# Query and key preparation of a grouped-query layer: a fixed order over three tiles, doubled key heads, and score steps between the last products

## The chip, the cores and the metric

One Trainium2 chip, one of its cores. The metric is the device time of one execution in microseconds (us), lower is better. Times of several runs are given as median, lowest and highest; one more execution is profiled, and all rows of the profile are from that one.

The five engines run in parallel, each through its own list of instructions, in order: TensorE (PE; its weight loads are shown as PEld), VectorE (DVE), ScalarE (ACT), GpSimd (POOL) and SyncE (SP), which issues most DMA transfers. ScalarE's list issues DMA transfers too (ACTq). Matmuls write to PSUM, which has eight banks; GpSimd works on SBUF alone here.

## What is computed

One step of a two-layer trunk: 512 latent tokens and 128 context tokens ("prompt"), 1,024 channels, 16 heads of 64. Layer 0 mixes by neighbourhood attention, layer 1 by grouped-query attention with 4 key and value heads, each layer followed by a gated convolutional feed-forward. All is float32. The change is in layer 1's mixer, cut to what matters:

```python
def gqa_qkv(h, w_qkv, q_norm, k_norm):
    q, k, v = jnp.split(h @ w_qkv, [1024, 1024 + 256], axis=-1)
    q = rmsnorm(q.reshape(b, t, 16, 64), q_norm)     # per head
    k = rmsnorm(k.reshape(b, t, 4, 64), k_norm)
    return q, k, v.reshape(b, t, 4, 64)

qp, kp, vp = gqa_qkv(hp, ...)                        # 128 context tokens
op = blocked_attention(qp, kp, vp)                   # context reads context
qs, ks_, vs = gqa_qkv(hs, ...)                       # 512 latent tokens
qs, ks_ = axial_rope(qs), axial_rope(ks_)            # latents carry a position
k_all = concat([ks_, cache_gqa_k], axis=1)           # 512 + 128 cached context keys
v_all = concat([vs, cache_gqa_v], axis=1)
os_ = blocked_attention(qs, k_all, v_all)
x = x + gate * rmsnorm(concat(op, os_) @ w_o, norm_mix_post)
```

The context's normed keys and its values are outputs too (new_gqa_k, new_gqa_v).

## The kernel before

**Precision.** A float32 product is made of three passes in a faster type: each operand is split into a high part (cast) and a low part (the rest), and high x high, high x low, low x high are summed in PSUM. `wsplit` loads a weight block (raw tile `wr`), casts it on ScalarE (`wh`) and subtracts on DVE or, where told so, on GpSimd (`wl`). Tag `wr`, `wh`, `wl` have four buffers each in the pool `wp`.

**Order.** The tile framework's scheduler orders the instructions of every engine and places the waits. Two things bind it. All matmuls and transposes go through `pe()`, which chains each behind the one before it: TensorE's order is the order of the program text. And `tc.keep_in_program_order(ins)` puts an instruction behind the one written last for the same engine. Before the change only the output projection's weight splits are pinned that way; the rest of DVE, ScalarE and GpSimd is ordered by the scheduler's estimate. A buffer that takes the place of an earlier one waits until that one is no longer read.

**Preparation of layer 1's heads.** There are 15 tiles of 128 tokens x 512 columns: five for keys and values (tile t = 0 to 3 latent, 4 context), five for the query heads 0 to 7 (`hq` 0; order 4, 0, 1, 2, 3) and five for heads 8 to 15 (`hq` 1; order 0 to 4). Each goes through these steps:

- products (`products`): 24 matmuls of 512 columns into one bank (`gp`), two weight blocks of 256 rows per six of them. `after(u)` is called behind each quarter, u = 0 to 3
- statistics (`head_rms`): ScalarE squares (`sq`), DVE sums per head (`ssh`), GpSimd makes variance and reciprocal root (`vh`, `rh`)
- norm (`head_norm`): DVE multiplies by the root (`y`) and by the rotary table (`tab`, into `kt` or `qt`), four small products give the rotated half (`sq` again), GpSimd adds the two. Context tiles (t = 4) need only two multiplies
- turn (`turn_k`, `turn_q`): transposes on TensorE into a bank (`tk`, `tq`), then casts on ScalarE to the high part and differences on DVE to the low part (`gkh`, `gkl`, `gq`). Two readers of one bank are kept apart by the framework: the second cast follows the first difference

Keys are needed twice in the partitions (once for each of the two heads that share a query block), so `turn_k` writes each half twice, in pieces of 64 partitions:

```python
        for j in range(2):
            turn(tp[:, j * P : j * P + P], src[:, j * P : j * P + P], ident)
        for b in range(2):
            for part in (own, oth):
                nc.scalar.copy(kh[part, b::2, cols], tv[own])
            for part in (own, oth):
                nc.vector.tensor_sub(kl[part, b::2, cols], tv[own], f32(kh[own, b::2, cols]))
```

The table `tab` is made by DVE from `rot` (the rotation) and `gn` (the two gains, each also with its quarters swapped), which ScalarE's list loads by seven transfers; two more load the cached keys and values (`ck`, `cv`). Their buffers lie where layer 0's closing norm had its own.

The driver `step` calls for each tile products and statistics, then the norm of the tile before, then turns that are older: with `keep` = 1 those of the tile two back, for key tiles (`KP` = 2, 2, 2, 2, 1) three back. All of it stands behind the whole tile's products. Query weights are split while the fifth tile of the group before is multiplied, one block behind each quarter. Between query tiles stand steps of the context's own attention (`gqa_prompt`: scores, turn, values), at the tiles listed in `PSTEP`, counted from the first query tile.

**The units.** Then come 32 units (`Unit`): one head and 256 latent queries each. `scores(i)`: four matmuls of 320 keys into two banks (`s`), minimum on DVE (`nmg`), exponential on ScalarE (into `gp`, the sums read out behind it), reciprocal on DVE (`rcg`), scaling on GpSimd. `turns(j)` transposes (`tp`) and evicts (`pk`), `values` multiplies with v (`po`). Scores run two units ahead; those of units 0 and 1 stand in front of the loop. The loop's steps are in `GORDER`; "p" takes a waiting prompt step. Units need the keys of all tiles, but query heads only as their number comes up.

Of the kernel before, what the change touches and what calls it, by code (L numbers as in the profile page):

```python
# [9 lines left out]
F32 = mybir.dt.float32  # L10
# [47 lines left out]
PSTEP = (3, 5, 6, 6, 8, 9)  # L58
WU = 29
TP = 1  # L60
PSN = 4
# [4 lines left out]
KP = (2, 2, 2, 2, 1)  # L66
# [35 lines left out]
def hybrid_step(ctx: ExitStack, tc: tile.TileContext, A, O):  # L102
# [1265 lines left out]
    def gqa_w(c0, u, low=None):  # L1368
        return wsplit(rows(wqkv, 2 * u, 2, c0, 512), 2, 512, low)
# [20 lines left out]
    rot = ap.tile([P, 2, 4, HD], F32, name="rot", bufs=1)  # L1390
    nc.scalar.dma_start(rot, A["k_rope"])
# [9 lines left out]
    tab = ap.tile([P, 2, 2, 4, HD], F32, name="tab", bufs=1)  # L1401
    for i in range(2):
        for j in range(2):
            nc.vector.tensor_mul(tab[:, i, j], rot[:, j], gn[:, i, j].unsqueeze(1).broadcast_to([P, 4, HD]))

    last_rms = [None]

    def head_rms(src, n):

        sq = ap.tile([P, 8, HD], F32, tag="sq", name="sq")[:, 0:n, :]  # L1410
        nc.scalar.activation(sq, src, AF.Square)
        ss = sm.tile([P, 8], F32, name="ssh")[:, 0:n]
        nc.vector.tensor_reduce(ss, sq, axis=AX.X, op=ALU.add)
        v = sm.tile([P, 8], F32, name="vh")[:, 0:n]
        nc.gpsimd.tensor_scalar(v, ss, 1.0 / HD, EPS, op0=ALU.mult, op1=ALU.add)
        r = sm.tile([P, 8], F32, name="rh")[:, 0:n]
        last_rms[0] = nc.gpsimd.tensor_tensor(r, v, mhalf.broadcast_to([P, n]), op=ALU.pow)
        return sq, r

    def head_norm(dst, src, sq, r, t, i, n):  # L1420

        y = ap.tile([P, 8, HD], F32, tag="y", name="y")[:, 0:n, :]
        nc.vector.tensor_mul(y, src, r.unsqueeze(2).broadcast_to([P, n, HD]))
        if t == 4:
            nc.vector.tensor_mul(dst, y, gn[:, i, 0].unsqueeze(1).broadcast_to([P, n, HD]))
            return
        nc.vector.tensor_mul(dst, y, tab[:, i, 0, t].unsqueeze(1).broadcast_to([P, n, HD]))
# [3 lines left out]
        for b in range(2):  # L1431
            for a in range(2):
                nc.vector.tensor_mul(
                    s5[:, :, a, b, :], y5[:, :, a, 1 - b, :],
                    b4[:, a, b, :].unsqueeze(1).broadcast_to([P, n, 16]),
                )
        nc.gpsimd.tensor_add(dst, dst, sq)

    def put_v(c, src):
        nc.scalar.copy(vt[:, c], src.rearrange("p (a d) -> p a d", a=4))  # L1440

    def turn_k(src, cols):

        tp = bk.get("tk")
        for j in range(2):
            turn(tp[:, j * P : j * P + P], src[:, j * P : j * P + P], ident)
        tv = tp[:, 0:256].rearrange("p (a b) -> p a b", a=2)
        for b in range(2):
            own, oth = own_oth(b)
            for part in (own, oth):  # L1450
                nc.scalar.copy(kh[part, b::2, cols], tv[own])
            for part in (own, oth):
                nc.vector.tensor_sub(kl[part, b::2, cols], tv[own], f32(kh[own, b::2, cols]))
# [354 lines left out]
```

## Time and profile before

| | |
|---|---|
| median of 3 runs | 1630.63 us (1628.24 to 1637.93) |
| profiled execution | 1631.72 us, span 1629.9 us |
| mean granted TensorE clock | 0.986 |
| busy over the span | PE 96%, DVE 62%, ACT 53%, POOL 44% |
| stage of preparation | 874.7 to about 984 us |
| units | about 984 to 1125 us |

How to read the rows. A timeline row is start, duration, engine, line, operation, output <- input, count, and in brackets how long the engine was idle before and who ended that. A group's row has busy time, mean duration in ns, idle time before its instructions and its releaser; a tile's row has minimum, median and maximum duration in ns, then first and last start. A waits row is who waited, on whom, us in total, times, longest. A windows row has for a stretch of time the busy us and instructions of each engine, the granted TensorE clock (1.00 is full), the DMA share and GB/s. Matmuls overlap: a duration of 0.39 us goes with a start every 0.23 us.

### The profile page before, as it was taken

To read this page: it belongs to the slowest core of one execution; us is meant where nothing else is said; L and a number is where in the kernel's file an instruction comes from. 1 tells how busy PE (TensorE), PEld (TensorE's weight loads), DVE (VectorE), ACT (ScalarE), POOL (GpSimd) and SP (SyncE) were. 2 spreads that over 40 slices of the span, in tenths; PEclk is the share of its full clock that TensorE was granted. 3 is DMA by queue.
4 is the path that set the end of the run, shared out by engine and by line. 5 is a ranking of instruction groups with operands and counts; after the bars stand their busy time and mean duration, and the time that the engine had idled before them with its cause. 6 is when DMAs were issued, how large, how long until landed. Compare 5 with 4: busy or idle time off the path is not lost.

```text
span 1629.9 us, 26039 instructions
## 1 busy us (share of the span) xinstructions
PE 1557.0 (96%) x9709; PEld 1350.8 (83%) x9709; DVE 1011.8 (62%) x1645; ACT 858.0 (53%) x1641; POOL 723.0 (44%) x614
## 2 busy tenths in 40 slices
PE   5999999899999999999999997999999999999998
PEld 3888889778888888998887776777898999998886
DVE  3453534549866565775465877773787888885454
ACT  3464646545545454554444445763565656565433
POOL 1554545423253544544343355441524556563333
PEclk8999999999999999999999999999999999999999
DMA  9745553245466666348575110002635333338664
GB/s 286 184 138 143 137 143 73 63 135 176 147 199 214 196 204 207 103 161 299 197 235 178 60 39 14 1 1 101 220 114 187 117 103 109 107 115 285 209 210 140
DMA packets 193211, 242.42 MB, mean 149 GB/s; under 512 B 11100, under 2 KB 149564, under 8 KB 193084
## 3 DMA queue, kind: packets, MB, share of 16 engines
q1 hardware_dynamic: 182224, 233.13, 45.2%
q10 hardware_dynamic: 10860, 7.62, 2.7%
q8 instruction: 76, 1.25, 0.3%
q14 instruction: 51, 0.42, 0.1%
HBM read 214.38 MB, written 26.34 MB: 148 GB/s over the span
## 4 chain that ended last, share of the span: by engine, by line
PE 65%; DVE 12%; POOL 6%; DMA 6%; issue 5%; ACT 4%; SPq 1%; ACTq 0%; POOLq 0%; DVEq 0%
PE acc L114 18%; PE ux L114 10%; PE y L114 7%; PE qk L114 5%; PE uz L114 5%; PE s L114 4%; PE po L114 4%; PE tp L117 3%; PE vp L114 3%; DMA wr<-in_ada_w 3%; PE uy L114 3%; POOL wl L1099 2%; PE ada L114 2%; DVE t L1175 2%; DVE al L1099 1%
## 5 line engine op out<-in xcount | busy, mean ns | idle before, releaser
L167 POOL TENSOR_TENSOR wl<-wr,wh 128x1024 fp32r<-128x1024 f32 x75 | 183.7, 2452 | 267.1 <-ACT wh L165 260.6
L1099 POOL TENSOR_TENSOR wl<-wr,wh 128x1024 fp32r<-128x1024 f32 x80 | 194.6, 2451 | 55.5 <-ACT wh L1098 46.2
L114 PE MATMUL ux<-B,wh 128*128 128x322 f32 x832 | 201.9, 313 | 1.7 <-DVE B L220 1.6
L1175 DVE SCALAR_TENSOR_TENSOR t<-C,cw,t 128x644 f32<-128x644 f32 x176 | 156.5, 889 | 57.4 <-ACT t L1173 56.6
L114 PE MATMUL acc<-wh,alo 128*128 128x512 f32 x440 | 172.0, 391 | 0.0
L114 PE MATMUL acc<-wh,ahi 128*128 128x512 f32 x440 | 171.9, 391 | 0.0
L114 PE MATMUL acc<-wl,ahi 128*128 128x512 f32 x440 | 171.8, 391 | 0.0
L165 ACT CAST wh<-wr 128x1024 fp32r<-128x1024 f32 x140 | 145.3, 1048 | 32.9 <-DMA wr<-in_ffn_w_down 23.9
L114 PE MATMUL uz<-B,wh 128*128 128x322 f32 x640 | 158.5, 316 | 0.0
L114 PEld LDWEIGHTS ux<-B,wh 128*128 128x128 f32 x832 | 143.7, 189 | 9.4 <-issue 2.9
L1068 DVE TENSOR_TENSOR alo<-ain,ahi 128x384 fp32r<-128x384 f32 (+1 forms) x88 | 70.9, 815 | 95.7 <-ACT ahi L1066 95.4
L114 PE MATMUL ux<-B,wl 128*128 128x322 f32 x416 | 129.1, 310 | 0.0
L114 PE MATMUL qk<-hT,wh 128*128 128x384 f32 (+1 forms) x512 | 126.0, 319 | 0.3 <-DVE qs L776 0.2
L114 PEld LDWEIGHTS uz<-B,wh 128*128 128x128 f32 x640 | 111.8, 190 | 6.6 <-issue 3.7
L1099 POOL TENSOR_TENSOR vl<-wr,vh 128x1024 fp32r<-128x1024 f32 x38 | 96.8, 2547 | 36.4 <-ACT vh L1098 36.4
L1098 ACT CAST wh<-wr 128x1024 fp32r<-128x1024 f32 x88 | 89.6, 1050 | 33.1 <-DVE wr L1122 31.8
L1066 ACT CAST ahi<-ain 128x384 fp32r<-128x384 f32 (+1 forms) x88 | 40.2, 461 | 124.8 <-PE acc L114 91.7
L1173 ACT ACTIVATE t<-C,cw 128x644 f32<-128x644 f32 x88 | 78.7, 895 | 48.5 <-DVE C L1203 44.3
L114 PE MATMUL uz<-B,wl 128*128 128x322 f32 x320 | 100.2, 313 | 0.5 <-POOL wl L1099 0.4
L167 DVE TENSOR_TENSOR wl<-wr,wh 128x1024 fp32r<-128x1024 f32 x65 | 83.5, 1299 | 25.0 <-ACT wh L165 24.5
L114 PEld LDWEIGHTS acc<-wl,ahi 128*128 128x128 f32 x440 | 82.6, 188 | 18.0
L114 PEld LDWEIGHTS acc<-wh,ahi 128*128 128x128 f32 x440 | 82.6, 188 | 17.7
(249 smaller groups left out, 4009.4 us busy)
## 6 DMA issues: line engine op xcount, KB each, us to landing
wr<-in_ffn_w_up SPq DMA_DIRECT2D x88, 512.0 KB
wr<-in_ffn_w_down SPq DMA_DIRECT2D x88, 512.0 KB
wr<-in_ada_w SPq DMA_DIRECT2D x80, 512.0 KB
act<-act SPq DMA_DIRECT2D x44, 321.0 KB
wr<-in_na_w_qkv SPq DMA_DIRECT2D x24, 512.0 KB
mod<-modrow SPq DMA_DIRECT2D x20, 512.0 KB
ain<-act SPq DMA_DIRECT2D x44, 192.0 KB
wf<-in_ada_w SPq DMA_DIRECT2D x16, 512.0 KB
```

Source lines behind the costliest of these rows:

```text
L114: pe(nc.tensor.matmul(*a, **k))
L117: pe(nc.tensor.transpose(*a, **k))
L165: i = nc.scalar.copy(hi, raw)
L167: j = (low or nc.vector).tensor_sub(lo, raw, f32(hi))
L1066: nc.scalar.copy(hi[:, 0 : c1 - c0], ain[:, 0 : c1 - c0])
L1068: nc.vector.tensor_sub(lo[:, 0 : c1 - c0], ain[:, 0 : c1 - c0], f32(hi[:, 0 : c1 - c0]))
L1098: nc.scalar.copy(hl[0], src)
L1099: low.tensor_sub(hl[1], src, f32(hl[0]))
L1173: nc.scalar.activation(t, taps(0), AF.Identity, bias=cw[:, 3, n : n + 1], scale=cw[:, 1, n : n + 1])
L1175: nc.vector.scalar_tensor_tensor(t, taps(d), cw[:, w, n : n + 1], t, op0=ALU.mult, op1=ALU.add)
```

## The change

- The tile's steps become a class `Prep` with `products`, `stat`, `norm`, `turns`, and one loop runs over the 15 tiles. While tile i is multiplied, behind its first quarter: `stat` of i-1, `turns` of i-2 (and behind tile 2's first quarter also the cached keys' turn). Behind its last: `norm` of i-1. Every instruction of these steps on DVE, ScalarE and GpSimd is pinned (`o` is `tc.keep_in_program_order`).
- Query weight blocks are split earlier and pinned: block 0 of heads 0 to 7 behind tile 1, on GpSimd and in a pool of its own (`wx`); block 0 of heads 8 to 15 behind tile 6 (block 1 of these then takes `wx`); the others behind the first two quarters and the end of tiles 4 and 9, one of them on GpSimd.
- Keys: the norm writes each head twice side by side (`twice`), the cached keys are loaded twice; four transposes give both halves, then one cast and one difference over 128 partitions.
- The four score steps of units 0 and 1 move between the products of tiles 12 to 14 (`ESC`: tile and quarter to unit and step). Their exponentials go to `wr` buffers. The score banks are opened at tile 12, and the last 4 of the other banks are dropped there.
- Prompt steps stand at other tiles (`PSTEP` now counts from the first key tile). The last tile's turn and the opening of the attention output's buffers move behind unit 1.
- `rot` is loaded into a part of `tab`; the cached values are loaded straight to `vt`, without a copy.

```diff
-PSTEP = (3, 5, 6, 6, 8, 9)
+PSTEP = (8, 9, 10, 10, 11, 12)
+ESC = {(12, 2): (0, 0), (13, 1): (0, 1), (13, 3): (1, 0), (14, 2): (1, 1)}
-PSN = 4
-KP = (2, 2, 2, 2, 1)
...
+    o = tc.keep_in_program_order
     def head_rms(src, n):
-        nc.scalar.activation(sq, src, AF.Square)
+        o(nc.scalar.activation(sq, src, AF.Square))
...
-    def head_norm(dst, src, sq, r, t, i, n):
+    def head_norm(dst, src, sq, r, t, i, n, twice=None):
-        nc.vector.tensor_mul(y, src, r.unsqueeze(2).broadcast_to([P, n, HD]))
+        o(nc.vector.tensor_mul(y, src, r.unsqueeze(2).broadcast_to([P, n, HD])))
...
-        nc.gpsimd.tensor_add(dst, dst, sq)
+        if twice is not None:
+            dst, sq = (x.unsqueeze(2).broadcast_to([P, n, 2, HD]) for x in (dst, sq))
+        o(nc.gpsimd.tensor_add(dst if twice is None else twice, dst, sq))
...
     def turn_k(src, cols):
         tp = bk.get("tk")
-        for j in range(2):
-            turn(tp[:, j * P : j * P + P], src[:, j * P : j * P + P], ident)
...
+        for g in range(4):
+            turn(tp[:, g * P : g * P + P], src[:, g].rearrange("p a b -> p (a b)"), ident)
+        tv = tp.rearrange("p (a b) -> p a b", a=4)
+        o(nc.scalar.copy(kh[:, :, cols], tv))
+        o(nc.vector.tensor_sub(kl[:, :, cols], tv, f32(kh[:, :, cols])))
         bk.put(tp)
...
-    ck = ap.tile([P, 256], F32, tag="ck", name="ck", bufs=1)
-    nc.scalar.dma_start(ck, A["cache_gqa_k"][0, 0].rearrange("t h d -> t (h d)"))
-    cv = ap.tile([P, 256], F32, tag="cv", name="cv", bufs=1)
-    nc.scalar.dma_start(cv, A["cache_gqa_v"][0, 0].rearrange("t h d -> t (h d)"))
+    ck = ap.tile([P, 4, 2, HD], F32, name="ck", bufs=1)
+    for b in range(2):
+        nc.scalar.dma_start(ck[:, :, b, :], A["cache_gqa_k"][0, 0])
+    nc.scalar.dma_start(vt[:, 5], A["cache_gqa_v"][0, 0])
...
+    tiles = [Prep(None, t) for t in range(NT)]
+    tiles += [Prep(hq, t) for hq in range(2) for t in ((4, 0, 1, 2, 3), (0, 1, 2, 3, 4))[hq]]
+    group = [wkv, [], []]
+    for i, x in enumerate(tiles):
+        g = i // NT
+        def after(u):
+            if u == 0:
+                if i:
+                    tiles[i - 1].stat()
+                if i > 1:
+                    tiles[i - 2].turns()
+                if i == 2:
+                    turn_k(ck, slice(NS, T))
+            if i % NT == 4 and g < 2:
+                if u < 2:
+                    group[g + 1].append(gqa_w(512 * g, u + 1, (None, nc.gpsimd)[u], wx if g and u == 0 else None, True))
+            if (i, u) in ESC:
+                v, j = ESC[i, u]
+                if v not in un:
+                    un[v] = Unit(v)
+                un[v].scores(j)
+        if i == 10:
+            bk.first = psx
+        if i == 12:
+            bk.drop(4)
+            psy.close()
+            sps_p.append(sps.enter_context(pool("pss", space=PSUM)))
+        x.products(group[g], i % NT == 0, after)
+        if i:
+            tiles[i - 1].norm()
+        if i % NT == 4 and g < 2:
+            group[g + 1].append(gqa_w(512 * g, 3, None, None, True))
+        if i == 0:
+            late[0]()
+        elif i == 1:
+            late[1]()
...
+            group[1].append(gqa_w(0, 0, nc.gpsimd, wx, True))
+        elif i == 6:
+            group[2].append(gqa_w(512, 0, nc.gpsimd, None, True))
+        elif i == 7:
+            extra.extend(gqa_prompt(0) + gqa_prompt(1))
+        for _ in range(PSTEP.count(i)):
+            extra.popleft()()
+    bk.first = None
+    extra.extend(gqa_prompt(2) + gqa_prompt(3))
+    tiles[-1].stat()
+    tiles[-2].turns()
+    tiles[-1].norm()
...
-        for u in range(2):
-            for i in range(2):
-                un[u].scores(i)
         for u in range(NU + 2):
+            if u == 2:
+                tiles[-1].turns()
...
-                    if extra and (u == 0 or u >= PU0):
+                    if extra and u >= PU0:
                         extra.popleft()()
```

More of the change, by code (lines that the diff above doesn't have):

```diff
@@ L1389, in hybrid_step @@
     ap = gqs.enter_context(pool("gp", 2, "right"))
-    rot = ap.tile([P, 2, 4, HD], F32, name="rot", bufs=1)
-    nc.scalar.dma_start(rot, A["k_rope"])
+    wx = gqs.enter_context(pool("wx", 1, "right"))
+    tab = ap.tile([P, 2, 2, 4, HD], F32, name="tab", bufs=1)
+    nc.scalar.dma_start(tab[:, 1], A["k_rope"])
     gn = ap.tile([P, 2, 2, HD], F32, name="gn", bufs=1)
@@ new lines, in values @@
+    def values(two, cs):
+        u = two[0]
+        if cs[0] == 0 and u.hf == 0:
+            ta["po"] = bk.get("po")
+        for c in cs:
+            for v in two:
+                mm(ta["po"][64 * v.b : 64 * v.b + 64, 256 * u.hf : 256 * u.hf + 256],
+                   vt[:, c if c < 4 else 5, u.g, :], v.t[c], start=c == 0, stop=c == 4)
+        if cs[-1] == 4 and u.hf == 1:
+            p = u.p
+            hi, lo = osp1[p]
+            nc.scalar.copy(hi[:, 0:NS], ta["po"])
+            nc.vector.tensor_sub(lo[:, 0:NS], ta["po"], f32(hi[:, 0:NS]))
+            bk.put(ta["po"])
+            c, src = slice(NS, T), opr[:, p, :]
+            if p == KC - 1:
+                nc.scalar.copy(hi[:, c], src)
+                nc.vector.tensor_sub(lo[:, c], src, f32(hi[:, c]))
+            else:
+                i = nc.gpsimd.tensor_scalar(hi[:, c], src, 1.0, None, op0=ALU.mult)
+                nc.gpsimd.tensor_sub(lo[:, c], src, f32(hi[:, c]))
+                tc.add_manual_dep(i.ins, last_rms[0].ins.name, no_sync, reason="order")
@@ L1572, in hybrid_step @@
             late[0]()
-        elif t == 1:
+        elif i == 1:
             late[1]()
             xmp.close()
+            l_q = ExitStack()
+            lastq = l_q.enter_context(pool("q14", 1))
             pp_s = ExitStack()
             cur = [pp_s.enter_context(pool("prp", 1))]
-    turns.append(lambda: turn_k(ck, slice(NS, T)))
-    put_v(5, cv)
-    extra = deque()
-    for hq in range(2):
-        for n, t in enumerate(((4, 0, 1, 2, 3), (0, 1, 2, 3, 4))[hq]):
-            if hq and n == PSN:
-                bk.first = psx
-            step(q_tile(t, hq, wqs[hq], n == 0, ahead_of(1) if 5 * hq + n == 4 else None))
-            i = 5 * hq + n
-            if n == 2:
-                extra.extend(gqa_prompt(2 * hq) + gqa_prompt(2 * hq + 1))
-            for _ in range(PSTEP.count(i)):
-                extra.popleft()()
@@ L1591, in hybrid_step @@
-    step()
-    extra.extendleft(turns)
+            group[1].append(gqa_w(0, 0, nc.gpsimd, wx, True))
[10 more added lines that the diff above has]
+    tiles[-1].norm()
     pp_s.close()
-    hp2.close()
@@ L1595, in hybrid_step @@
     gqs.close()
     l_o1 = ExitStack()
-    op1 = l_o1.enter_context(pool("o1"))
-    osp1 = [[op1.tile([P, T], F32R, name=f"p{i}{p}") for i in "hl"] for p in range(KC)]
-    bk.first = None
-    bk.drop(4)
-    psy.close()
+    osp1 = []
     with ExitStack() as s:
```

234 lines of the change are left out of this document (103 added, 131 removed).

## The prediction

> **What bounds the kernel now.** I read the page for the span, then the windows of the stage between the last feed-forward product of layer 0 (874.7 us) and the steady grouped-query units (from 1002 us), then TensorE's waits there, then the engines' timelines. Outside this stage the change moves nothing of weight.
>
> ```profile
> span 1629.9 us, 26039 instructions
> ```
>
> TensorE waited here for this (us in total, times, longest):
>
> ```profile
> PE s L114 <- ACT gp L1635: 6.9, 3, 5.6
> PE tq L117 <- POOL qt L1437: 4.2, 2, 2.3
> PE gp L114 <- ACT wh L165: 3.6, 2, 1.9
> PE tk L117 <- POOL kt L1437: 2.0, 2, 1.8
> PE gp L114 <- DVE wl L167: 0.4, 1, 0.4
> PE po L114 <- DVE gq L1466: 0.3, 1, 0.3
> ```
>
> Together 17.4 us: the first scores, which wait for the exponentials of the first units (6.9), turns of queries and keys that wait for GpSimd's last addition (6.2), query weights (3.6), 0.7 of rest. Idle time also costs clock. Three waits on TensorE's timeline (the wait in brackets, the last one in layer 1's feed-forward):
>
> ```profile
> 943.60 5.55 PE L114 MATMUL gp<-wh,hT 128*128 128x512 f32 x16 [1.93 <-ACT wh L165]
> 990.67 0.90 PE L114 MATMUL s<-gkh,gq 128*128 128x320 f32 x2 [5.56 <-ACT gp L1635]
> 1250.35 0.64 PE L114 MATMUL ada<-wr,scolp 128*32 128x256 f32 x8 [3.26 <-DMA wr<-in_ada_w]
> ```
>
> and the windows behind them:
>
> ```profile
> core 0: us, PE busy (x) PEld busy (x) DVE busy (x) ACT busy (x) POOL busy (x), PEclk, DMA share, GB/s
> 943.00:949.00 6.00, 5.40 (x17) 4.22 (x18) 5.81 (x7) 4.35 (x6) 3.28 (x2) 0.72 0.03 4
> 990.00:996.00 6.00, 5.33 (x21) 4.93 (x21) 3.75 (x8) 3.64 (x9) 2.38 (x3) 0.50 0.12 18
> 1250.00:1254.00 4.00, 3.65 (x28) 3.24 (x29) 2.96 (x6) 2.75 (x5) 1.40 (x2) 1.00 0.23 86
> ```
>
> At clock 0.72 a window loses 6 x 0.28 = 1.7 us, at 0.50 it loses 5.33 x 0.5 = 2.7. So the stage loses 17.4 + 1.7 + 2.7 = 21.8 us, and no better order can gain more: 1.3%.
>
> **The change part by part.** TensorE's instructions are chained in the order written, before and after. What moves is where each turn stands in it, and what DVE must do ahead.
>
> *The first key turn.* Before, tile 0's keys are turned after tile 3's products (the list KP lets turns lag); now a quarter into tile 2's. They need the rotary table, whose loads ScalarE issues:
>
> ```profile
> 874.73 3.87 PE L114 MATMUL gp<-wh,hT 128*128 128x512 f32 x16
> 878.44 1.73 PE L114 MATMUL gp<-wl,hT 128*128 128x512 f32 x6
> 884.28 0.34 ACTq L1391 DMA_DIRECT2D rot<-in_k_rope  x1
> 888.36 0.48 PE L114 MATMUL gp<-wh,hT 128*128 128x512 f32 x1
> 893.25 0.23 DVE L1400 TENSOR_SCALAR gn<-gn 128x128 f32<-128x128 f32 x1 [5.32 <-DMA gn<-in_gqa_q_norm]
> 896.52 0.43 DVE L1404 TENSOR_TENSOR tab<-rot,gn 128x256 f32<-128x256 f32 x1 [1.58 <-DMA gn<-in_gqa_k_norm]
> 897.11 0.41 ACT L1440 COPY gvt<-cv 128x256 f32<-128x256 f32 x1 [6.02 <-DMA cv<-in_cache_gqa_v]
> 899.21 0.73 POOL L1437 TENSOR_TENSOR kt<-kt,sq 128x256 f32<-128x256 f32 x1 [0.55 <-DVE sq L1433]
> 900.00 0.44 PE tk L117 x2
> ```
>
> The last row is from the chain of waits. Sixteen products take 3.71 from start to start (878.44 - 874.73), one 0.23. Tile 2's start at 888.36; six of them put the turn at 889.75. The table is there at 896.95 and the turned tile was ready at 900.0. The loads stay where they are in the program and their space still comes from the same buffers of the feed-forward, so I leave the time: a hole of 10.2 us. GpSimd's addition now writes heads twice, 512 wide (1.29 instead of 0.73), DVE has less of other tiles in between: 899.6 to 900.6. Right behind stands the turn of the cached keys. Before they came as 128 lines of 1 KB; now twice, 1,024 pieces of 256 bytes. k_norm's three loads are 640 small pieces and landed 3.3 us (896.52 - 893.25) behind q_norm's; at that rate 1,024 take 5.2 us, to 901.7, while the first turn ends at 900.4. I take 1.0, between 0 (they land with the rest, at 897.1) and 2. The Trainium skill ("DMA: Bandwidth & Descriptors", Specifications) puts line rate at pieces of 512 bytes or more. [...]
>
> *Query tiles.* A tile's turn now comes one quarter into the second tile after it. Turn to turn takes 6.0 us, 0.43 of it the turn (6.0 - 24 x 0.232):
>
> ```profile
> 967.04 0.60 PE L117 MATMUL tq<-ident,qt 128*128 128x128 f32 x4
> 973.04 0.60 PE L117 MATMUL tq<-ident,qt 128*128 128x128 f32 x4
> 974.51 0.89 DVE L1433 TENSOR_TENSOR sq<-y,tab 128x128 f32<-128x128 f32 x4
> L1466 DVE TENSOR_TENSOR gq<-tq,gq 64x512 fp32r<-64x512 f32 x9 | 6.2, 688 | 0.3
> L1465 ACT CAST gq<-tq 64x512 fp32r<-64x512 f32 x10 | 5.8, 577 | 10.6 <-DVE gq L1466 7.9 <-PE tq L117 2.6
> L1437 POOL TENSOR_TENSOR qt<-qt,sq 128x512 f32<-128x512 f32 x5 | 6.4, 1281 | 8.1 <-DVE sq L1433 8.1
> L1423 DVE TENSOR_TENSOR y<-gp,rh 128x512 f32<-128x512 f32 x4 | 2.8, 692 | 8.3 <-POOL rh L1417 8.3
> ```
>
> The new order on DVE is: statistics of i-1, the two low parts of i-2's turn, then the norm of i-1. The second cast waits for the first low part (the ScalarE row's wait), so from a turn to DVE being free: 0.60 + 2 x (0.58 + 0.69) + four hops of 0.04 = 3.3. From the norm's start to the next turn: two multiplies of 0.69 (the y row), the four of the rotation, GpSimd's addition: 0.69 + 0.69 + 0.89 + 1.28 + 0.2 of hops = 3.75. Sum 7.05: longer than 6.0, so a plain tile waits 1.05, unless prompt steps fill it. Two tiles have weight splits pinned ahead:
>
> ```profile
> L167 POOL TENSOR_TENSOR wl<-wr,wh 128x1024 fp32r<-128x1024 f32 x75 | 183.7, 2452 | 267.1 <-ACT wh L165 260.6
> L167 DVE TENSOR_TENSOR wl<-wr,wh 128x1024 fp32r<-128x1024 f32 x65 | 83.5, 1299 | 25.0 <-ACT wh L165 24.5
> ```
>
> Tile 6: 1.05 + 0.8, GpSimd's split (2.45) now stands ahead of its variance. Tile 8: DVE's split (1.3) stands ahead of its norm: 7.05 + 1.5 less 6.35 (a prompt step) = 2.2. Tile 10: 0.7. Tile 3, behind GpSimd's split: 1.0. Tiles 7 and 9 lie beside a prompt's scores: 0. Sum 5.8.
>
> *Early scores.* Four score steps go between the last products. Each is four matmuls, a minimum, an exponential, a reciprocal:
>
> ```profile
> 959.90 0.65 PE L114 MATMUL po<-ptp,gvt 128*64 128x256 f32 x4
> 983.70 0.53 PE L114 MATMUL s<-gkh,gq 128*128 128x320 f32 x2
> 984.07 0.46 PE L114 MATMUL s<-gkl,gq 128*128 128x320 f32 x2
> L1634 DVE TENSOR_REDUCE nmg<-s x64: 806/824/827, 988.9 to 1108.8; 128x1 f32<-128x640 f32 x64
> L1635 ACT ACTIVATE gp<-s,nmg x64: 786/796/827, 989.7 to 1109.7; 128x640 f32<-128x640 f32 x64
> L1635 ACT ACTIVATION_READ_ACCUMULATOR gp<-s,nmg x64: 190/193/229, 990.4 to 1110.4; 128x1 f32 x64
> 990.65 0.16 DVE L1637 RECIPROCAL rcg<-sug 128x1 f32<-128x1 f32 x1 [0.22 <-ACT gp L1635]
> ```
>
> The score is done 0.83 after its start (984.07 + 0.46 - 983.70) and holds TensorE 0.7; then 0.82 + 0.80 + 0.19 + 0.16 + hops = 2.1. The norm that follows is pinned behind the reciprocal, DVE is in order, so the norm waits for the exponential, and behind it the low parts and the next turn. Counted from a turn: scores after the third quarter end at 0.4 + 12 x 0.23 + 0.83 = 4.0, the next turn is ready at 4.0 + 2.1 + 3.75 = 9.85. TensorE gets there at 6.0 + 0.7 + 0.55 (a prompt's values, the first row) = 7.25: **2.6**. In tile 13, with two score steps, the second at its end: 0.4 + 1.4 + 0.7 + 2.8 + 0.83 + 2.1 + 3.75 = 12.0 against 7.4: **4.6**. Behind tile 14 the turn of 13 follows at 0.4 + 18 x 0.23 + 0.7 = 5.3: **4.5**. Sum 11.7. If the reciprocal didn't stand ahead, the three would be 0, 0 and 1.8.
>
> *Clock.* The hole of 10.2 costs the 2.7 of the 990 window. Those of 4.5 and 4.6 lie between a wait of 3.26, after which the clock stayed at 1.00, and 5.56, after which it was 0.50; one of 1.93 gave 0.72. Between 0 and 2.7 each, I take 1.7. Sum 6.1. The Trainium skill ("TensorE: Matmul & The Clock Gate", HAM oscillation) wants no idle gap over about 3.4 us and gives a cold phase of one such window at half rate: estimated from it, 1.7 for each of three holes, 5.1. The 1.93 row speaks against its threshold.
>
> *The rest.* Doubled heads turn four blocks instead of two, six times: 12 more transposes at 0.11 (0.43 a turn of four), +1.3. DVE saves three of four low parts a key turn, but they lie beside products: 0. The wait of 0.4 for the first weights stays. The 3.6 for query weights goes: splits are written a tile earlier. The 6.9 at the first scores goes: they are done when the last products are. Their place is taken by TensorE's queue behind the turn of tile 13 (priced above), then 0.5 for units meeting the last low parts on DVE (0 to 3). The last turn moves behind two units: 0. The weight buffers that the first units now hold are wanted by the output weights, needed 100 us later: 0.
>
> After: 0.4 + 11.2 + 5.8 + 11.7 + 6.1 + 1.3 + 0.5 = 37.0; before: 21.8. **+15.2 us**, on the profiled execution's 1631.7 (1.8 around the span; 1.1 over the median of the runs): 1646.9, and against the median **1645.8**.
>
> **The rivals.** *Worse:* half clock behind every hole above 1.9 (tiles 8 and 11 too, +4 with 2.7 at the two of 4.5, +2), cached keys at 901.7 or later (+1), unit minima behind the last tile's norm (+2): 1655. For it: 1.93 already dropped the clock once; against: 3.26 didn't. *The tables come in time:* ScalarE had nothing to do before this:
>
> ```profile
> 881.77 0.59 ACT L399 CAST hT<-tr 128x512 fp32r<-128x512 f32 x1 [4.40 <-PE tr L117]
> ```
>
> If the loads were issued in that gap, at 877.4, 6.9 earlier, the hole would be 3.3 and its clock loss gone: 15.2 - 6.9 - 2.7 = +5.6, 1636. Against it: in the trace even the cached keys' load was queued behind the tables. *Faster, the chain doesn't bind:* in the gap between two turns. If the scheduler's order or the hardware let the norm's chain run 9.8 - 7.25 shorter (it decides at TensorE's 7.25), the holes of query tiles are nil: 15.2 - 11.7 - 5.8 - 3.4 = -5.7, 1625. For it: before, turns between 961 and 979 us wait for nothing; against: there they had six microseconds more. *The pins change little* because the scheduler already had this order: the trace before has key turns behind tile 3's products, so no; only as no net change, in the cases above.
>
> **How the numbers follow.** The likeliest sum has chance 0.5, spread over 1638 to 1652; worse 0.27 (1648 to 1660); tables in time 0.10 (1630 to 1640); chain not binding 0.13 (1608 to 1630). One per cent is 16.3 us, about what a measurement of this kernel can tell from no change; 1647 is that line, and the likeliest case stands on it. Slower by over 1%: 0.20 of the likeliest and 0.26 of worse, 0.46; faster by over 1% needs nearly all of the 21.8: 0.06; within: 0.48. The range leaves 0.1 on each side: 1626 to 1657.
>
> **What would show it.** Right: TensorE idle some 10 us near 890, ended by GpSimd's addition to the doubled keys; half clock behind it; waits of turns for that addition at the last three query turns, longest 4 to 5; DVE's norm idle until a reciprocal; the 5.6 at the first scores gone. Wrong: table loads landing before 890; query norms ahead of the reciprocals; TensorE busy through the query tiles.

## The result, and the profile after

The changed kernel takes **1654.95 us** (median; 1651.77 to 1658.2), the kernel before 1630.28 (1628.24 to 1637.93): ratio 1.014, 95% interval 1.0113 to 1.0167, so 18 to 27 us slower. The profiled execution of after took 1658.2 us (span 1656.4, mean clock 0.976).

What TensorE waited for in the stage, from the waits of after (us in total, times, longest):

```profile
PE tq L116 <- POOL qt L1444: 16.9, 6, 4.5
PE tk L116 <- POOL kd L1444: 14.0, 2, 11.3
PE tp L116 <- DVE gq L1469: 1.3, 1, 1.3
PE s L113 <- ACT gp L1593: 1.0, 2, 0.8
PE gp L113 <- DVE wl L166: 0.4, 1, 0.4
```

33.6 us where there were 17.4. The 6.9 at the first scores and the 3.6 for query weights are gone (1.0 and nothing); in their place turns wait for GpSimd's last addition, 30.9 in all. The single waits on TensorE's timeline, between the first product of the stage and the units' first values:

```profile
877.22 3.87 PE L113 MATMUL gp<-wh,hT 128*128 128x512 f32 x16
...
903.81 1.11 PE L116 MATMUL tk<-ident,kd 128*128 128x128 f32 x4 [11.31 <-POOL kd L1444]
904.71 0.63 PE L116 MATMUL tk<-ident,ck 128*128 128x128 f32 x2
...
927.39 0.66 PE L116 MATMUL tk<-ident,kd 128*128 128x128 f32 x4 [2.69 <-POOL kd L1444]
...
946.42 0.66 PE L116 MATMUL tq<-ident,qt 128*128 128x128 f32 x4 [0.85 <-POOL qt L1444]
...
964.67 1.11 PE L116 MATMUL tq<-ident,qt 128*128 128x128 f32 x4 [4.49 <-POOL qt L1444]
...
982.39 0.66 PE L116 MATMUL tq<-ident,qt 128*128 128x128 f32 x4 [0.85 <-POOL qt L1444]
...
992.10 0.66 PE L116 MATMUL tq<-ident,qt 128*128 128x128 f32 x4 [2.15 <-POOL qt L1444]
...
1003.78 0.67 PE L116 MATMUL tq<-ident,qt 128*128 128x128 f32 x4 [4.29 <-POOL qt L1444]
...
1015.06 1.11 PE L116 MATMUL tq<-ident,qt 128*128 128x128 f32 x4 [4.31 <-POOL qt L1444]
...
1024.85 1.51 PE L113 MATMUL po<-pk,gvt 128*64 128x256 f32 x12
```

In this order: the first key turn (11.31; the cached keys right behind it wait for nothing), the turns of tiles 3, 6, 8, 10, and the last three, 11, 12 and 13. From the first row to the last the stage takes 147.6 us; before it took 127.8 (874.73 to 1002.56). That is 19.8 of the difference, and the 1.3 at the first `tp` lies just behind the last row. The windows behind five of the waits:

```profile
core 0: us, PE busy (x) PEld busy (x) DVE busy (x) ACT busy (x) POOL busy (x), PEclk, DMA share, GB/s
903.80:912.00 8.20, 8.19 (x30) 6.89 (x31) 2.91 (x9) 1.72 (x4) 4.78 (x4) 0.70 0.22 66
927.00:935.00 8.00, 7.61 (x37) 6.34 (x38) 2.76 (x6) 2.47 (x5) 2.79 (x5) 1.00 0.37 113
964.60:972.00 7.40, 7.33 (x24) 5.72 (x24) 3.57 (x8) 1.17 (x2) 2.98 (x4) 0.62 0.00 0
1003.70:1011.00 7.30, 6.97 (x26) 5.42 (x26) 2.20 (x3) 1.89 (x4) 1.87 (x3) 0.77 0.01 2
1015.00:1023.00 8.00, 6.96 (x42) 6.46 (x43) 6.08 (x11) 4.47 (x10) 6.50 (x13) 0.82 0.26 77
```

Busy time times the missing clock: 8.19 x 0.30 + 7.33 x 0.38 + 6.97 x 0.23 + 6.96 x 0.18 = 8.1 us. Behind the wait of 2.69 the clock stayed full.

**The first key turn.** From the timelines of ScalarE's queue and VectorE in after: the table's loads and what waits for them.

```profile
885.70 0.35 ACTq L1391 DMA_DIRECT2D tab<-in_k_rope  x1
...
891.13 0.39 ACT L1411 ACTIVATE sq<-gp 128x256 f32<-128x256 f32 x1 [4.31 <-DMA tab<-in_k_rope]
...
898.28 0.43 DVE L1403 TENSOR_TENSOR tab<-tab,gn 128x256 f32<-128x256 f32 x1 [1.67 <-DMA gn<-in_gqa_k_norm]
898.62 0.41 DVE L1413 TENSOR_REDUCE ssh<-sq 128x4 f32<-128x256 f32 x1
```

ScalarE's first square stands behind the issuing of the loads, VectorE's first sum (`ssh`) behind the last table multiply, and the addition comes at 902.5.

**The last three query turns.** VectorE's timeline in after has each norm right behind a reciprocal, which waits for an exponential:

```profile
988.22 0.16 DVE L1595 RECIPROCAL rcg<-sug 128x1 f32<-128x1 f32 x1 [0.95 <-ACT gp L1593]
988.30 0.67 DVE L1423 TENSOR_TENSOR y<-gp,rh 128x512 f32<-128x512 f32 x1
```

The other two have the same pair at 999.91 and 1011.19.

**Tiles 3 and 8.** Here something shows that no row of this stage showed before, where the longest table multiplies took 0.69 us (queries) and 0.50 (keys). The table multiplies of the stage in after, one row for each of its tiles, qt and kt (ns: minimum, median, maximum):

```profile
L1432 DVE TENSOR_TENSOR qt<-y,tab x8: 691/753/2037, 943.5 to 1012.0; 128x512 f32<-128x512 f32 x8
L1432 DVE TENSOR_TENSOR kt<-y,tab x4: 417/425/2187, 901.4 to 922.4; 128x256 f32<-128x256 f32 x4
```

and the longest of them on the timelines of the two engines:

```profile
921.76 2.50 POOL L166 TENSOR_TENSOR wl<-wr,wh 128x1024 fp32r<-128x1024 f32 x1 [2.10 <-ACT wh L164]
922.36 2.19 DVE L1432 TENSOR_TENSOR kt<-y,tab 128x256 f32<-128x256 f32 x1
925.01 1.21 DVE L166 TENSOR_TENSOR wl<-wr,wh 128x1024 fp32r<-128x1024 f32 x1
925.17 2.17 POOL L1444 TENSOR_TENSOR kd<-kt,sq 128x512 f32<-128x512 f32 x1 [0.90 <-DVE sq L1438]
```

The multiply that takes 0.42 us elsewhere took 2.19, started inside GpSimd's low part and ended at 924.55, 0.29 behind that low part's end. Then GpSimd's addition (1.29 elsewhere) took 2.17, started inside VectorE's low part, and ended 1.12 behind its end. Tile 8 repeats both: 2.04 instead of 0.69, 2.18 instead of 1.26.

### The profile page after: what moved, and what is told of

Its sections match the earlier page's. It is cut to its first block, busy times and chain, and to the rows that moved or that the text cites. A ratio compares the mean times of both kernels' runs of the same rounds, so it can differ in the third digit from the quotient of the medians.

```text
span 1656.4 us, 26017 instructions
## 1 busy us (share of the span) xinstructions
PE 1566.5 (95%) x9721; PEld 1359.3 (82%) x9721; DVE 1010.8 (61%) x1624; ACT 854.2 (52%) x1622; POOL 736.5 (44%) x618
## 4 chain that ended last, share of the span: by engine, by line
PE 51%; DVE 9%; POOL 5%; DMA 5%; issue 3%; ACT 3%; ACTq 0%; POOLq 0%; SPq 0%; DVEq 0%
PE acc L113 18%; PE ux L113 10%; PE uz L113 5%; DMA wr<-in_ada_w 3%; PE y L113 3%; PE uy L113 3%; PE gp L113 3%; POOL wl L1098 2%; PE po L113 2%; PE s L113 2%; PE tp L116 2%; DVE al L1098 1%; DVE t L1174 1%; PE ada L113 1%; POOL vl L1098 1%
## 5 line engine op out<-in xcount | busy, mean ns | idle before, releaser
L166 POOL TENSOR_TENSOR wl<-wr,wh 128x1024 fp32r<-128x1024 f32 x79 | 193.7, 2454 | 272.2 <-ACT wh L164 265.6
L1098 POOL TENSOR_TENSOR wl<-wr,wh 128x1024 fp32r<-128x1024 f32 x80 | 194.7, 2452 | 59.5 <-ACT wh L1097 50.1
L1067 DVE TENSOR_TENSOR alo<-ain,ahi 128x384 fp32r<-128x384 f32 (+1 forms) x88 | 75.3, 866 | 88.3 <-ACT ahi L1065 87.4
L113 PEld LDWEIGHTS acc<-wh,alo 128*128 128x128 f32 x440 | 82.5, 188 | 17.7
```

Of the source, the lines that this page charges most:

```text
L113: pe(nc.tensor.matmul(*a, **k))
L166: j = (low or nc.vector).tensor_sub(lo, raw, f32(hi))
L1067: nc.vector.tensor_sub(lo[:, 0 : c1 - c0], ain[:, 0 : c1 - c0], f32(hi[:, 0 : c1 - c0]))
L1098: low.tensor_sub(hl[1], src, f32(hl[0]))
```

## Experiments

All kernels but one (noted there) start from the changed kernel or from the one with its chains cut. *Stage* is the time from the first key and value product to the first value product of the units, in the profiled execution; it does not see how the layers before and behind vary from run to run. *Ratio* is the time over the kernel before on the same chip, with its 95% interval.

| kernel | stage, us | median, us | ratio |
|---|---|---|---|
| before | 127.8 | 1630 to 1633, by the chip | 1 |
| after | 147.6 | 1654.95 | 1.0140 (1.0113 to 1.0167) |
| late key turns | 144.8 | 1648.82 | 1.0093 (1.0060 to 1.0126) |
| table out of the way | 140.9 | 1643.83 | 1.0083 (1.0055 to 1.0111) |
| norms ahead of scores | 136.1 | 1642.92 | 1.0055 (1.0034 to 1.0077) |
| no pins | 136.4 | 1640.94 | 1.0054 (1.0035 to 1.0072) |
| no early scores | 142.6 | 1647.84 | 1.0103 (1.0079 to 1.0127) |
| low parts exchanged | 145.4 | 1649.42 | 1.0104 (1.0061 to 1.0146) |
| first three together | 131.3 | 1637.24 | 1.0039 (1.0019 to 1.0059) |
| single heads | 148.7 | 1656.83 | 1.0149 (1.0121 to 1.0177) |
| before + doubled heads | 131.6 | 1635.61 | 1.0028 (1.0011 to 1.0046) |
| chains cut | 123.0 | 1627.51 | 0.9971 (0.9955 to 0.9986) |
| chains cut, single heads | 129.8 | 1637.10 | 1.0026 (1.0011 to 1.0041) |
| chains cut, turn 13 moved | 125.5 | 1630.64 | 0.9986 (0.9971 to 1.0001) |

"First three together" is late key turns, norms ahead of scores and low parts exchanged. *Clock lost*, below, is TensorE's busy time times the missing clock, summed over the stage in windows of 1 us: 8.3 us in after, 4.4 in before. In the seven kernels from late key turns to first three together, the change of TensorE's waits and of the clock lost gives the change of the stage against after to within 0.6 us.

**Late key turns.**

```diff
-                if i > 1:
-                    tiles[i - 2].turns()
-                if i == 2:
+                if i > 3:
+                    tiles[0 if i == 4 else i - 2].turns()
+                if i == 4:
                     turn_k(ck, slice(NS, T))
+            if i == 4 and u in (1, 2):
+                tiles[u].turns()
```

> The changed kernel, with the key turns moved: no turn beside tiles 2 and 3; tile 0's keys and the cached keys are turned a quarter into tile 4, tile 1's and 2's at its next two quarters. Theory (the turn stands ahead of the tables, which are ready only at 903.8 us): the wait of 11.3 us and the half clock behind it (2.5) go, waits at the key turns come to 1 us at most together, nothing else changes: 13.8 less than the changed kernel's 1655, so 1641 (1638 to 1645), and TensorE's waits in the stage come to about 22 instead of 33.6. Rival 1 (the hole only moves: the norms of the key tiles all come late, so the turns of tiles 1 and 2 and those of the first query tiles wait in its place): waits in the stage stay above 28 and the time above 1648. Rival 2 (the time comes from doubled heads and more transposes): 1655, as the transposes are the same.

The ratio fell to 1.0093, some 8 us below after, with intervals that overlap; in the stage, where the edit acts, 2.8 of the expected 13.8 came. The wait of 11.3 went, but other turns wait now, so that the waits fell by 5.3 only, to 28.3, and the clock lost rose from 8.3 to 11.0. From the timelines of TensorE, ScalarE and GpSimd in this kernel, in order of time:

```profile
899.82 2.39 POOL L166 TENSOR_TENSOR wl<-wr,wh 128x1024 fp32r<-128x1024 f32 x1
899.90 0.38 ACT L1411 ACTIVATE sq<-gp 128x256 f32<-128x256 f32 x1 [9.63 <-POOL kd L1444]
899.92 0.66 PE L116 MATMUL tk<-ident,kd 128*128 128x128 f32 x4 [0.40 <-POOL kd L1444]
...
902.29 0.20 POOL L1415 TENSOR_SCALAR vh<-ssh 128x4 f32<-128x4 f32 x1
...
906.50 1.11 PE L116 MATMUL tk<-ident,kd 128*128 128x128 f32 x4 [4.10 <-POOL kd L1444]
...
918.58 0.66 PE L116 MATMUL tk<-ident,kd 128*128 128x128 f32 x4 [3.56 <-POOL kd L1444]
```

Tile 1's variance (902.29) stands behind tile 0's addition and, pinned between them, a low part of 2.39; tile 2's square waited 9.6 us, though its products were long done, until that addition freed one of two `sq` buffers. So behind the late table stood a chain, pinned and short of buffers. The first rival is right by its own figures (waits above 28, a time above 1648) and for the key turns; the first query turns wait no longer than in after.

**The table out of the way.**

```diff
-    nc.vector.tensor_scalar(gn[:, 0], ...)      # and the four tab multiplies: now behind tile 2's norm
...
-        o(nc.vector.tensor_mul(dst, y, tab[:, i, 0, t]...))
+        o(nc.vector.tensor_mul(dst, y, y))      # key tiles; likewise the four products of the rotated half
...
-                if i == 2:
+                if i == 3:
                     turn_k(ck, slice(NS, T))
```

> The changed kernel, whose key tiles 0 to 3 are multiplied by themselves instead of by the rotary table (this leaves their rotation out), with as many multiplies of the same shapes; the table is worked out on VectorE behind tile 2's norm, when its loads have long landed, and the cached keys are turned beside tile 3. Theory (of the first key turn's wait of 11.3 us the table is the part from ScalarE's first square to the last table multiply, and ScalarE's issuing of the loads ahead of that square is the rest): the square starts at the same place, about 14 us after the first key and value product, statistics, norm and addition take 5 behind it, so the doubled keys are ready 19 us after that product instead of 26.6 and the wait is 3 to 4; 7.7 and about 1 of clock less than 1655, so 1646 (1643 to 1650). Rival (GpSimd's additions and its first low part hold the key turns): waits of key turns stay at 12 or more in all, 1652 to 1656.

The stage lost 6.7 us. ScalarE's first square and the first key turn on their timelines:

```profile
888.73 0.39 ACT L1407 ACTIVATE sq<-gp 128x256 f32<-128x256 f32 x1 [4.88 <-DMA gn<-in_gqa_q_norm]
...
894.34 1.12 PE L116 MATMUL tk<-ident,kd 128*128 128x128 f32 x4 [4.83 <-POOL kd L1443]
```

The turn came 20.1 us behind the stage's first product (894.34 - 874.24) instead of 26.6 (903.81 - 877.22), with 4.8 of wait instead of 11.3. The table, with the statistics that stand behind its last multiply, is 6.5 of the 11.3; the rest is statistics, norm and addition behind a square that ScalarE starts late. That square starts as late as in after (14.5 us behind the first product, 13.9 there), behind the issuing of the loads on ScalarE; that the issuing holds it is read from the rows, and no kernel took it away.

**Norms ahead of the early scores.**

```diff
+            if i >= 12 and u == 1:
+                tiles[i - 1].norm()
             if (i, u) in ESC:
...
-        if i:
+        if 0 < i < 12:
             tiles[i - 1].norm()
```

> The changed kernel, with the norms of tiles 11, 12 and 13 written a quarter into the next tile, ahead of the early score steps instead of behind them; the scores stay where they are. Theory (the norms stood behind the reciprocals on VectorE, which wait for the exponentials): the waits at the last three query turns fall from 2.15, 4.29 and 4.31 to about 0.5, 0.5 and 1.8, the clock behind them is whole (2.9 less), the units' start costs up to 1 more because the minima now stand behind the norms: 9 to 11 less than 1655, so 1645 (1643 to 1648). Rival (the chain of low parts, norm and GpSimd's addition is too long for one tile by itself): waits of 2 and more stay at each of the three and the time is 1651 to 1655.

Some 14 us below after by the ratios, 11.5 in the stage. The three turns on TensorE's timeline:

```profile
987.20 0.66 PE L116 MATMUL tq<-ident,qt 128*128 128x128 f32 x4 [0.24 <-POOL qt L1444]
994.90 0.66 PE L116 MATMUL tq<-ident,qt 128*128 128x128 f32 x4 [0.31 <-POOL qt L1444]
1002.78 0.66 PE L116 MATMUL tq<-ident,qt 128*128 128x128 f32 x4 [2.46 <-POOL qt L1444]
```

10.75 us of waits become 3.0, and the clock lost falls by 1.9. It was the place of the norm behind the reciprocal, not the length of the chain.

**No pins.**

```diff
-    o = tc.keep_in_program_order
+    o = lambda x: x
```

> The changed kernel with the fixed order of the preparation given up on VectorE, ScalarE and GpSimd (the weight splits keep theirs); TensorE's instructions, early scores and turns stand where they did. The order that the scheduler then writes has the norms of tiles 11 to 13 ahead of the reciprocals and both low parts of tiles 4 and 9 together. Theory (pins cost what they put behind a reciprocal, the first key turn does not depend on them): waits at the last three query turns 0.5, 0.5 and 2 to 3 instead of 2.15, 4.29 and 4.31, the first key turn's wait stays at 10 to 11: 10 less than 1655, so 1645 (1641 to 1649). Rival 1 (the pins change little): 1653 to 1657. Rival 2 (the pins bring something elsewhere that is lost): above 1657.

Theory held: the first key turn still waits 11.25, the stage is 11.2 shorter. The scheduler puts the late norms ahead of the reciprocals by itself, and the last three turns wait 3.3 instead of 10.75 in all; the turns of tiles 3 and 8 no longer wait (7.2 in after), some 6 us of waits elsewhere are new, and the clock lost is 2.4 less. So the pinned order as written costs the 11, not the pinning, and not all of it at the last norms.

**No early scores.**

```diff
-ESC = {(12, 2): (0, 0), (13, 1): (0, 1), (13, 3): (1, 0), (14, 2): (1, 1)}
+ESC = {}
...
     tiles[-1].norm()
+    for v in (0, 1):
+        un[v] = Unit(v)
+        for j in (0, 1):
+            un[v].scores(j)
```

> The changed kernel with the four early score steps taken back out: the first two units' scores follow the last tile's norm, as in the kernel before; all else as changed. Theory (a norm behind a reciprocal is what the waits at the last query turns are; the scores' place was to save the 6.9 us at the first scores): the waits at the turns of tiles 11 and 12 fall from 2.15 and 4.29 to 0.3 each, the one of tile 13 to 2 to 3, and 5 to 7 come back where the first scores wait for exponentials, with their 2.7 of clock: 4 less than 1655, so 1651 (1647 to 1654), and 8 above the 1643 of the kernel with norms ahead of the scores. Rival (early scores give nothing even with the norms ahead): the waits at the first scores do not come back, and the time is 1643.

5 us of the stage less than after, 6.5 more than with the scores kept and the norms ahead of them. So the early place is worth 6 to 7 us once nothing is pinned behind it: 3.0 of waits and 3.3 of clock lost, in these two profiles. But the first scores waited 2.3 in all, not 5 to 7: that part of my expectation was wrong, and why the 5.6 of the kernel before did not come back was not tried.

**Low parts exchanged.**

```diff
-  group[g + 1].append(gqa_w(512 * g, u + 1, (None, nc.gpsimd)[u], ...))
+  group[g + 1].append(gqa_w(512 * g, u + 1, None, ...))
...
-            group[g + 1].append(gqa_w(512 * g, 3, None, None, True))
+            group[g + 1].append(gqa_w(512 * g, 3, nc.gpsimd, None, True))
```

> The changed kernel, with the low parts of two weight units exchanged in tile 4 and in tile 9: the second one on VectorE instead of GpSimd, the last one on GpSimd (behind its addition) instead of VectorE. Each engine has as much work as before. Theory (VectorE's multiplies with two operands in SBUF stand still while GpSimd writes a low part, and GpSimd's addition runs at half speed beside VectorE's low part): the key multiply falls from 2.19 us to 0.42 and the query multiply from 2.04 to 0.69, the additions from 2.17 to 1.29; the turns behind them wait 1.3 less each (2.69 to 1.4, 4.49 to 3.2), and with up to 2.8 of clock the time is 3 to 5 less than 1655. Rival (the long multiplies come from the semaphores they wait for, not from GpSimd): they stay at 2 us, and the time within 1 of 1655.

The same groups in this kernel:

```profile
L1432 DVE TENSOR_TENSOR qt<-y,tab x8: 691/692/824, 940.3 to 1009.0; 128x512 f32<-128x512 f32 x8
L1432 DVE TENSOR_TENSOR kt<-y,tab x4: 417/426/427, 900.6 to 921.8; 128x256 f32<-128x256 f32 x4
L1444 POOL TENSOR_TENSOR qt<-qt,sq x8: 1260/1264/1295, 942.0 to 1010.8; 128x512 f32<-128x512 f32 x8
L1444 POOL TENSOR_TENSOR kd<-kt,sq x4: 1260/1277/1300, 901.7 to 923.0; 128x512 f32<-128x512 f32 x4
```

No maximum is above 1.3 us any more, with the same work on both engines: the two held each other. The turns of tiles 3 and 8 waited 1.21 and 3.47 (2.69 and 4.49), the stage is 2.2 shorter. The time's interval (1.0061 to 1.0146) overlaps after's, so the gain stands on the rows and not on the time.

**The three together.** 

> All three edits of this call together: late key turns, norms ahead of the scores, exchanged low parts. Theory (three separate causes): the three gains add, 13.8 + 10 + 4 = 28 less than 1655, so 1627 (1624 to 1633), about the time of the kernel before. Rival (one bound shared by all, such as VectorE's chain from tile to tile, takes over): 1635 to 1645.

1637: 131.3 in the stage, 16.3 less than after, where the three alone took 2.8, 11.5 and 2.2, so they add (16.5). The 28 failed mainly at the late key turns (2.8 for 13.8), a little at the low parts (2.2 for 4); key turns still wait 7.9. The time is the rival's, but its reason, one bound shared by all, does not fit gains that add.

**Single heads, and doubled heads alone.** The first undoes one part of the change, the second does it alone on the kernel before (with `rot` loaded into `tab`, as in the change).

```diff
-        for g in range(4):
-            turn(tp[:, g * P : g * P + P], src[:, g]..., ident)
-        o(nc.scalar.copy(kh[:, :, cols], tv))
-        o(nc.vector.tensor_sub(kl[:, :, cols], tv, f32(kh[:, :, cols])))
+        (the two transposes, four casts and four low parts of before, pinned)
```

> The changed kernel with one part undone: keys are turned in single heads, two transposes per turn, with four casts and four low parts, and cached keys are loaded once in 1 KB lines; the table's place in memory, the order, the splits and the early scores as changed. Theory (doubled heads are worth about nothing here): 12 transposes and the wider addition less (1.3 and 0.6), against three more low parts per key turn on VectorE ahead of the norms (0.5 to 1 at the turn of tile 3): 1654 (1651 to 1657). Rival 1 (doubled heads cost what the kernel before with doubled heads alone had more): 1650 or less. Rival 2 (they save VectorE's time where it is the chain): above 1658.

> The kernel before with one part of the change alone: heads of keys doubled, both copies turned at once, one cast and one low part per key turn, cached keys loaded twice, and the table multiplied in place to make room; order, norms, splits and scores as before. Theory (doubled heads cost 12 transposes of 0.11 us and hardly anything else): 1 to 2 more than the kernel before's 1632, so 1633 (1630 to 1636), waits of key turns about 2 as before. Rival (the wider additions on GpSimd, 1.29 us instead of 0.73, and the cached keys in 256-byte pieces hold the turns up): 5 or more above the kernel before, with waits of key turns of 5 and more.

In the changed order, doubled or single makes no difference that the time can tell. Alone, doubling made the kernel before slower, 0.1 to 0.5%. That is not the heads' work alone: there ScalarE issued the table's loads 12.0 us behind the first product instead of 9.6, and the first key turn waited 5.5. The tiles lie elsewhere in memory there, which may be why; it was not tried. These two runs leave the heads' own price open; a later one measures it in a better order.

**The chains cut.** Late key turns, and:

```diff
+        if i < 4:
+            x.stat()                    # ahead of the norm of tile i-1, not behind it
+        if i == 1:
+            group[1].append(gqa_w(0, 0, nc.gpsimd, wx, True))   # ahead of tile 0's addition
...
-        sq = ap.tile([P, 8, HD], F32, tag="sq", name="sq")[:, 0:n, :]
+        sq = ap.tile([P, 8, HD], F32, tag="sq", name="sq", bufs=3)[:, 0:n, :]
...
+            if i >= 4 and u == 1:
+                tiles[i - 1].norm()     # ahead of the scores, and of the low parts of tiles 4 and 9
```

> The changed kernel with late key turns as in the first call, and the chains found there cut: the statistics of the key tiles stand ahead of the norm that waits for the table, with three buffers for the squares instead of two; GpSimd's first low part stands ahead of the first addition; from tile 4 on each norm is written a quarter into the next tile, ahead of that tile's scores and of the weights' low parts. Theory (with late turns alone the wait moved because tile 1's and 2's statistics were pinned behind tile 0's norm, and GpSimd's low part behind its addition): the waits of key turns fall from 7.9 in the kernel with the first three edits to 2 at most, the one behind the splits of tile 9 from 3.5 to about 1, with 3 to 4 of clock: 10 to 12 less than 1637, so 1626 (1622 to 1630), 6 below the kernel before. Rival (GpSimd's own work, additions, splits and variances one behind the other, bounds the key tiles): waits of key turns of 5 and more remain, 1632 to 1637.

1627.5, ratio 0.9971 (0.9955 to 0.9986): faster than after by some 28 us and than before by 2 to 7. TensorE's waits in the stage of this kernel:

```profile
PE tq L117 <- POOL qt L1445: 7.5, 7, 2.5
PE tk L117 <- POOL kd L1445: 2.2, 2, 1.7
PE s L114 <- ACT gp L1594: 1.6, 1, 1.6
PE tp L117 <- DVE gq L1470: 1.3, 1, 1.3
```

With two rows of 0.4 more it is 13.4, where after had 33.6 and before 17.4; no wait is longer than 2.5. TensorE has the same 9,721 instructions as in after: the 28 us (24.6 of them in the stage) were order and one buffer. What each of the cuts did alone was not tried.

**The same with single heads** (the edit of the single heads above).

> The kernel with the chains cut, with keys turned in single heads (two transposes, four casts, four low parts per key turn; cached keys loaded once). Without the hole at the first key turn the doubled heads are seen alone. Theory (they are worth about nothing): 12 transposes of 0.11 and the wider addition less, against three more low parts and casts for each of four turns close together in tile 4, which push tile 3's norm and the splits behind it back by 1 to 3: a ratio to the kernel before of 0.997 to 0.999, against 0.9971 with doubled heads. Rival 1 (doubling costs): 0.995 or less. Rival 2 (doubling frees VectorE where it counts): 1.000 or more.

Rival 2 is right and my "worth nothing" wrong: 0.55% or 9 us, 6.8 of it in the stage. VectorE's and TensorE's timelines in this kernel:

```profile
908.14 1.73 DVE L1461 TENSOR_TENSOR gkl<-tk,gkh 64x256 fp32r<-64x256 f32 x4 [0.82 <-ACT gkh L1459]
910.68 1.73 DVE L1461 TENSOR_TENSOR gkl<-tk,gkh 64x256 fp32r<-64x256 f32 x4 [0.81 <-ACT gkh L1459]
...
914.19 1.22 PE L114 MATMUL gp<-wh,hT 128*128 128x512 f32 x2 [3.12 <-ACT wh L165]
```

Casts and low parts of one bank take turns, so one key turn takes 2.5 us here (910.68 - 908.14). Four of them in tile 4 hold ScalarE's weight casts, and TensorE waits 3.1 for those.

**Turn 13 moved into the units.**

```diff
-    tiles[-2].turns()
     tiles[-1].norm()
...
+            if u == 1:
+                tiles[-2].turns()
             if u == 2:
                 tiles[-1].turns()
```

> The kernel with the chains cut, and the turn of tile 13, which stood behind the last products with a wait of 2.5 us, moved into the units, one unit ahead of the last tile's turn; its heads are needed from unit 16 only. Theory (the wait is the place of the turn): the 2.5 go, the first units' waits (1.6 and 1.3) stay: 1.5 to 2.5 less, a ratio to the kernel before of 0.9955 to 0.9965. Rival (the first units wait for the exponentials instead, so that the end of the stage comes no earlier): 0.997 or more, with waits of 5 and more at the first units.

The rival, in kind: the wait moved. Tile 13's turn on TensorE's timeline:

```profile
989.70 1.09 PE L117 MATMUL tq<-ident,qt 128*128 128x128 f32 x4 [3.80 <-DVE y L1424]
```

The turn's bank waits for the last tile's norm (3.80), and the turn of tile 14, at 997.39, waits 2.35 for a low part. 0.9986 shows nothing gained over 0.9971.

## Why the prediction was right or wrong

The sign, the places and most of the mechanisms held; 1654.95 lies inside 1626 to 1657, 9 above 1645.8. Two things in this are luck. The sum is 6.0 short and not 8, because two of the terms err the other way: the hole +1.1, query tiles +3.1, clock +2.0, units +1.8, but cached keys -1.0 and scores -1.0. And the worse rival's 1655 meets the time almost exactly, although of its items only the half clock behind tile 8 and most of the units' 2 us came, and the largest part of the miss was in neither sum. Whether the change would be told from none was left open (0.46 for slower by over 1%, 0.48 for within); the interval lies above 1%.

By its terms (us, predicted and found in the trace of after):

| term | predicted | found |
|---|---|---|
| first weights | 0.4 | 0.4 |
| hole at the first key turn | 10.2 | 11.3 |
| cached keys behind it | 1.0 | 0 |
| tiles 3, 6, 8, 10 | 1.0, 1.85, 2.2, 0.7 | 2.69, 0.85, 4.49, 0.85 |
| early scores, turns 11, 12, 13 | 2.6, 4.6, 4.5 | 2.15, 4.29, 4.31 |
| clock | 6.1 | 8.1 |
| 12 more transposes | 1.3 | not measured alone |
| start of the units | 0.5 | 2.3 (0.85 + 0.16 + 1.29) |
| sum, less 21.8 of before | +15.2 | +21.2 |

- **The hole.** Right in its cause, the late table, shown by its removal (6.5 of the 11.3), and 1.1 short. Counted from the first product, the table's last multiply came 0.7 earlier than before (21.1 against 21.8 us), but tile 0's first sum, which stands behind that multiply now, stood ahead of it before. From VectorE's timeline in before:

```profile
894.53 0.41 DVE L1413 TENSOR_REDUCE ssh<-sq 128x4 f32<-128x256 f32 x1
```

So the addition starts 4.2 us behind the last multiply (902.49 - 898.28) instead of 2.7 (899.21 - 896.52). The pins do not make this order: without them the sum stands there too, at 898.86 behind 898.52.

- **Cached keys.** The doubled loads were in time: the row at 904.71 has no wait. That is no measure of their rate. The last gain's load had landed by 898.28, and 5.2 us more, as the prediction estimated, would still have been in time. The Trainium skill ("DMA: Bandwidth & Descriptors", Specifications) puts line rate at pieces of 512 bytes or more; what pieces of 256 bytes cost, no run here shows alone.
- **Early scores.** Sized within 0.5 each, and the counterfactual within 0.7: without the reciprocal ahead I had 0, 0 and 1.8, and the kernel with the norms first showed 0.24, 0.31 and 2.46.
- **The step that failed: query tiles.** I put the splits of tiles 3 and 8 into the sum as work that stands ahead. That they would hold the other engine's multiply and addition was not in the sum. The two turns waited 1.7 and 2.3 longer than in the sum; what the held multiply and the held addition in front of each took beyond their usual time comes to 2.6 (1.77 + 0.88) and 2.3 (1.35 + 0.92). The wait of 4.49 then cost 2.8 of clock that I had not counted. Exchanging the low parts took the held durations away whole, but the waits by 1.5 and 1.0 only; VectorE's second low part then stands ahead of the norm, which by the rows is the reason for the rest.
- **Clock.** The worse rival had half clock behind tile 8, and that came; behind the waits of 4.3 it cost 1.3 and 1.6, near the 1.7 taken. The Trainium skill ("TensorE: Matmul & The Clock Gate", HAM oscillation) warns of idle gaps above about 3.4 us. The five windows of after agree: 2.69 stayed at 1.00, those of 4.29 and more fell to 0.62 to 0.82. The 1.93 of before speaks against it, and so do other runs. Tile 3's wait of 2.69 left the clock at 1.00 in after, but at 0.72 in the kernel with the norms first (924.0 to 930.0). Tile 11's of 2.15 left it at 1.00 in after (992.1 to 998.1), but at 0.72 with late key turns (983.6 to 989.6). With the chains cut, 0.72 followed a wait of 1.72 (899.8 to 905.8). Each of these windows of 6 us lost up to 1.7. So in these runs waits of 1.7 to 2.7 us sometimes cost the clock and sometimes not, and one profile alone does not tell which will. The prediction took 1.7 for the first window of before from its whole 6 us; by the 5.40 busy it is 1.5, while windows of 1 us give 4.4 for both together, as it had.
- **Units.** Sized at 0.5 in a range of 0 to 3, found 2.3.
- **Rivals.** "Tables in time": no, the loads were issued at 885.70, 8.5 behind the first product. "The chain doesn't bind": it did, by 2.15 to 4.49. "The pins change little": taking them away gained 11.2 in the stage.
- **"Doubled heads: 0 for VectorE".** True of this order. In the order with the chains cut, the three saved low parts and casts per turn are worth 9 us.

The account gives 21.2 of the 22.8 us that the ratio 1.014 stands for, inside its interval (18 to 27); 1.3 of it, the transposes, is an estimate that no run measured alone.

## What to carry to other kernels

An order written by hand is only as good as the latest operand of each pinned instruction: everything behind it on that engine waits too, so ask of each pinned row what arrives last, and write what has its operands first. Here one change held its gain (scores in the products' shadow, fewer low parts) and its loss (norms behind reciprocals, statistics behind a late table) at once, and TensorE's list needed only its key turns moved to keep the first alone. When a wait is moved away, look for the second chain behind the first, pins and buffer counts, before taking the whole wait as gain.

## What the runs showed of the hardware

**VectorE and GpSimd hold each other.** A multiply of two SBUF operands on VectorE took 2.19 us instead of 0.42 and 2.04 instead of 0.69 while GpSimd wrote a low part; GpSimd's addition took 2.17 instead of 1.29 while VectorE wrote one. The multiply with one operand in PSUM (`y`) beside the same low part took its usual 0.42. The Trainium skill ("SBUF — State Buffer", SBUF: two separate sides) calls the pair of ports that the two engines share an exclusive lock: whoever starts first has it for the whole instruction, if VectorE reads two operands from SBUF, and the other waits. The trace agrees in both directions, to within 0.2 us: the held multiply ended 0.29 us behind the low part that held it (alone it takes 0.42), the held addition 1.12 behind (alone 1.29).
